# A diffusion layer's modulation: wider column blocks, another layout of the modulated streams, and earlier first loads

## The chip, the cores and the metric

The kernel runs on one core of a Trainium2 chip. The metric is the device time of one execution in microseconds, the median of several runs. Times of the profile come from one execution recorded by the hardware profiler. TensorE (PE in the profile, its weight loads PEld) does matmuls into PSUM; VectorE (DVE), ScalarE (ACT) and GpSimd (POOL) work on what lies in SBUF and, but for GpSimd, in PSUM. SP, ACT and POOL have queues of their own from which DMA transfers are issued, each in order.

## The reference, cut to what matters

One layer over 256 latent tokens `x` and 256 context tokens `ctx` of width 1024. Two conditioning vectors, `c` for the latent tokens and `c_ctx` for the context, give shift, scale and gate:

```python
mod_lat = jnp.split(jax.nn.silu(c) @ w_mod + b_mod, 6, axis=-1)      # w_mod: 1024 x 6144
mod_ctx = jnp.split(jax.nn.silu(c_ctx) @ w_mod + b_mod, 6, axis=-1)
sh1, sc1, g1, sh2, sc2, g2 = mod_lat
csh1, csc1, ... = mod_ctx
h_lat = rms_norm(x, norm_mix_g) * (1 + sc1) + sh1
h_ctx = rms_norm(ctx, norm_mix_g) * (1 + csc1) + csh1
y_lat = token_mixer(h_lat, h_ctx, ...)      # gated DeltaNet and GLA branches, both directions
x = x + g1 * y_lat
h = rms_norm(x, norm_ffn_g) * (1 + sc2) + sh2
x = x + g2 * moe_ffn(h, ...)                # top 4 of 32 experts, clamped SwiGLU
out = rms_norm(x, final_norm_g)
```

The first two vectors (`sh1`, `sc1`: columns 0 to 2047 of `w_mod`) are needed at once, for both streams. The other four (`g1`, `sh2`, `sc2`, `g2`: columns 2048 to 6143) are needed only after the mixer, and only for the latent stream.

## The kernel before, in words

All of it is float32; the projections run as three passes of fp32r halves. The program is written in the order of the layer, with two strings, ORDER1 and ORDER2, that give the order of the mixer's pieces by hand: `K0` is the DeltaNet key projection of head 0, `Pq0`, `Pk0`, `Pv0` are GLA projections, `U0` the GLA gates, `X0` the GLA attention, `V`, `Q`, `T`, `R` more of the same, and `M1` is one step of the rest of the modulation. A planner then orders the instructions of each engine and of each DMA queue: it takes the earliest in the program that its own costs say is ready. On the chip every engine and every queue runs in that order, and an instruction whose input is late holds all behind it.

**Beginning.** x and ctx are loaded, normalised and transposed (L218). The first modulation weights come in 16 loads of 512 KB, two halves `f` of eight k-tiles (L211), into a ring `wm` of eight buffers that the four `junk` tiles of the norm use too. Each load feeds two matmuls (L214) with the silu columns `sc` as stationary operand, 32 columns wide of which two are used; four column groups of the array take turns, so their sums lie in four groups of 32 rows of `pm`, and eight small matmuls with `sel` (L237) add them and turn them into columns `mc`. `modulate` (L167) then writes the modulated streams, 256 tokens each, as a high part (ScalarE, L171) and a low part (VectorE, L173 and L174) into `hT[0]` and `hT[1]`, with stream, k-tile and token as axes. Between the two halves stand three narrow loads of the low-rank projection (`wlr`, L226).

**Projections.** `wtake` loads 1024x128 weights into a ring of three buffers, `wsplit` makes the high and low halves on ScalarE and VectorE, and `passes` (L184) does 24 matmuls, of 512 columns where both streams are needed (K, V, Pk, Pv) and of 256 where only the latent one is.

**Rest of the modulation.** `wmod_next` (L849) is one step for 128 columns of `w_mod`: two loads of 256 KB from a ring `wm` of three buffers in the pool `ga`, eight matmuls with `sc` as stationary operand, four row groups of `pm`, a copy to SBUF by VectorE or ScalarE in turn, and in the next step a matmul with `sum4` (L879) that adds the four groups and turns the row into one column, which VectorE adds to the bias into `mod2` (L882, L884). There are 32 such steps, all in ORDER1.

**After that.** Closing `ga` makes room for `pD`, in which the DeltaNet's chunks are inverted (ORDER2); then the output projections, the router and the 32 experts, whose weights are prefetched into chunks as buffers come free.

Of the kernel before, what the change touches and what calls it, by code (L numbers as in the profile page):

```python
# [8 lines left out]
F32 = mybir.dt.float32  # L9
F32R = mybir.dt.float32r  # L10
# [3 lines left out]
AF = mybir.ActivationFunctionType  # L14
# [6 lines left out]
KT = 8  # L21
# [9 lines left out]
PF = (4, 0, 2, 0, 0, 1, 1, 0, 1, 0, 2, 1, 0)  # L31
DN = (0, 2, 1, 3)
HLB = (2, 2)
ORDER1 = "K0 Pq0 K1 Pk0 M1 U0 Pv0 Pv1 Pq1 Pk1 U1 M1 Pv2 M1 X0 M1 M1 M1 R0 M1 M1 K2 Pk2 Q0 M1 M1 Pq2 R1 M1 Pv4 M1 U2 Pq3 T0 M1 Pv3 X1 M1 M1 V0 Pv6 M1 Pv5 M1 T2 M1 T1 R2 M1 M1 Pk3 U3 V3 M1 V1 M1 Pv7 M1 X2 M1 R4 M1 K3 R3 M1 T3 V2 M1 R5 X3 Q1 Q2 R6 M1 M1 Q3 M1 R7 M1 M1"
ORDER2 = "A0 A0 G0 A0 A0 I0 I0 I0 I0 I0 I0 K4 G1 I0 K5 G3 G4 K6 G2 I0 G5 G6 K7 B0 B0 B0 B0 B0 B0 A1 T4 Q4 B0 A1 V4 Q6 V5 A1 A1 I1 T6 I1 T7 G7 I1 I1 T5 Z0 I1 I1 V6 H0 Q5 H1 Z1 I1 V7 I1 Q7 H2 B1 Z2 B1 B1 Z3 W0 B1 B1 B1 C1 Z4 Z5 H3 Z6 H4 B1 H5 H6 J0 Z7 Y0 Y1 Y2 H7 C1 Y3 C1"


# [1 line left out]
def hybrid_layer(ctx, tc, x, c, ctxt, c_ctx, w_mod, b_mod, norm_mix_g, norm_ffn_g, w_in, conv_w, a_log_f, a_log_b,  # L39
# [50 lines left out]
    big = open_pool("big")  # L90
    cst = open_pool("cst")
    lng = open_pool("lng")
    hT = [big.tile([128, 2, KT, 256], F32R, tag=f"hT{i}", name=f"hT{i}") for i in range(2)]
    xc = open_pool("xc")
    VA = xc.tile([16, 128], F32, name="VA")
    VR = xc.tile([96, 128], F32, name="VR")
    S.dma_start(VA[0:8], c[0].rearrange("(a p) -> a p", p=128))
# [2 lines left out]
    for src, tag in ((x, "yT"), (ctxt, "kA")):  # L100
        w = big.tile([128, 2, D], F32, tag=tag, name="xt" + tag)
        nc.sync.dma_start(w, src[0].rearrange("(t p) d -> p t d", p=128))
        xt += [w[:, 0], w[:, 1]]
    rows = [(b_mod[0], 24, 48), (norm_mix_g[0], 16, 8), (norm_ffn_g[0], 72, 8), (gla_gate_b_f[0], 80, 4),
            (gla_gate_b_b[0], 84, 4), (gla_norm_g[0], 88, 2), (gdn_norm_g[0], 90, 1)]
    for v_, r0, n in rows:
# [41 lines left out]
    xnT = [t_[:, k] for t_ in (big.tile([128, 4, 512], F32, tag=n, name="xn" + n) for n in ("yh", "yl")) for k in range(4)]  # L148
    rst = cst.tile([128, 4], F32, name="rst")
    for t in range(4):  # L150
        junk = xc.tile([128, D], F32, tag="wm", bufs=8, name=f"junk{t}")
        S.activation(junk, xt[t], AF.Square, accum_out=ss[:, t:t + 1])
    S.activation(rst, ss, AF.Ln, bias=epsc, scale=1.0 / D)
    S.activation(rst, rst, AF.Exp, scale=-0.5)
# [12 lines left out]
    def modulate(kt):  # L167
        hf_ = xc.tile([128, 512], F32, tag="hf", bufs=2, name=f"hf{kt}")
        for r in range(2):
            sl = slice(256 * r, 256 * r + 256)  # L170
            S.activation(hT[0][:, r, kt], xnT[kt][:, sl], AF.Identity, bias=mc[:, r, 0, kt:kt + 1],  # L171
                         scale=mc[:, r, 1, kt:kt + 1])
            V.tensor_scalar(hf_[:, sl], xnT[kt][:, sl], mc[:, r, 1, kt:kt + 1], mc[:, r, 0, kt:kt + 1], ALU.mult, ALU.add)  # L173
            V.tensor_sub(hT[1][:, r, kt], hf_[:, sl], hT[0][:, r, kt])  # L174

    def wraw(name):
        return lng.tile([128, KT, 128], F32, tag="w", bufs=3, name=name)
# [6 lines left out]
    def passes(p, hl, act, n, k0=0, k1=KT):  # L184


        for i, a in ((0, 0), (1, 0), (0, 1)):
            for kt in range(k0, k1):
                r = act[a][:, 0, kt] if n == 256 else act[a][:, :, kt]
                T.matmul(p if n == 256 else p.rearrange("p (a b) -> p a b", a=2), hl[i][:, kt], r,  # L190
                         start=i + a + kt == 0, stop=a == 1 and kt == KT - 1)

    def dense3(w, act, n, nm, then=None):
        hl = wsplit(w, nm)
# [12 lines left out]
    for f in range(2):  # L207
        pm = PJ([128, 512], f"pm0{f}")
        for kt in range(KT):
            w = xc.tile([128, 2, 512], F32, tag="wm", bufs=8, name=f"wm0{f}{kt}")  # L210
            nc.sync.dma_start(w, w_mod[0, kt * 128:(kt + 1) * 128, 0:2048].rearrange("p (s h n) -> p s h n", s=2, h=2)[:, :, f])  # L211
            for s in range(2):
                g_ = 32 * (2 * (kt % 2) + s)
                T.matmul(pm[g_:g_ + 32], sc[:, kt], w[:, s], start=kt < 2, stop=kt >= KT - 2)  # L214
            if f == 0:
                pt = TP([128, 512], f"xT{kt}")
                for t in range(4):
                    T.transpose(pt[:, 128 * t:128 * t + 128], xt[t][:, 128 * kt:128 * kt + 128], ident)  # L218
                V.tensor_copy(xnT[kt], pt)
            else:  # L220
                if kt == 3:

                    wl = wraw("wlr")
                    G.memset(wl, 0.0)
                    for c0, n, o in ((C_BETA, 16, 0), (C_A, 16, 32), (C_LR, 32, 64)):
                        nc.sync.dma_start(wl[:, :, o:o + n], w_in[0][:, c0:c0 + n].rearrange("(k p) n -> p k n", p=128))  # L226
                    lr = wsplit(wl, "lr")
                if kt >= 4:
                    modulate(kt - 4)
        if f:  # L230
            plr = PJ([128, 512], "plr")
            passes(plr, lr, hT, 512, 0, 4)
        mr = xc.tile([128, 512], F32, name=f"mr0{f}")
        V.tensor_copy(mr, pm)
        pt = TP([128, 4, 4], f"mt0{f}")
        for a in range(4):
            T.matmul(pt[:, a], mr[:, 128 * a:128 * a + 128], sel.rearrange("p s r -> p (s r)"), start=True, stop=True)  # L237
        fs = slice(4 * f, 4 * f + 4)
        V.tensor_tensor(mc[:, :, :, fs], pt.rearrange("p a (s r) -> p r s a", s=2),
                        vc[:, 24:40].rearrange("p (s a) -> p s a", s=2)[:, None, :, fs].to_broadcast([128, 2, 2, 4]), ALU.add)  # L240
        V.scalar_tensor_tensor(mc[:, :, 1, fs], mc[:, :, 1, fs], 1.0, vc[:, None, 16 + 4 * f:20 + 4 * f].to_broadcast([128, 2, 4]),
                               ALU.add, ALU.mult)
# [4 lines left out]
    for i in range(2):  # L247
        T.transpose(pt[:, i], CR[:, i], ident[0:108, 0:108])
    V.tensor_copy(cw.rearrange("p (t r) -> p t r", t=2), pt)
    close_pool("xc")  # L250

    alg = cst.tile([128, 16], F32, name="alg")
    dtb = cst.tile([128, 16], F32, name="dtb")
    for t_, pr in ((alg, (a_log_f, a_log_b)), (dtb, (dt_bias_f, dt_bias_b))):
        for i in range(2):
            nc.sync.dma_start(t_[:, 8 * i:8 * i + 8], dap(pr[i], 0, [[0, 128], [1, 8]]))

    def dense(src, col, act, n):
        return dense3(wtake(src, col), act, n, f"{src.tensor.name}{col}")

    def proj(col, n):
        return dense(w_in, col, late.get("hact", hT), n)

    passes(plr, lr, hT, 512, 4, KT)
    lrr = cst.tile([96, 512], F32, name="lrr")
# [521 lines left out]
    def spare(_):  # L787

        h1 = big.tile([128, KT, 256], F32R, tag="ra", name="hc1")
        S.copy(h1, hT[1][:, 0])  # L790
        mix = big.tile([128, 2, KT, 256], F32R, tag="hT1", name="mix")
        S.copy(mix[:, 0], hT[0][:, 0])
        late["mix"] = mix[:, 1]
        late["hact"] = mix[:, 0:1], h1[:, None]

# [43 lines left out]
    G.memset(gl_static["A"], 0.0)  # L839
    G.memset(gl_static["B"], 0.0)  # L840
    mod2 = keep.tile([128, 4, 8], F32, name="mod2")
    sum4 = cst.tile([128, 1], F32, name="sum4")
    V.tensor_reduce(sum4, ident[:, 0:128:32], AX.X, ALU.add)
    b1c = cst.tile([128, 8], F32, name="b1c")
    V.tensor_scalar_add(b1c, vc[:, 56:64], 1.0)

    wms = [0]

    def wmod_next(n):  # L849

        for _ in range(n):
            k, wms[0] = wms[0], wms[0] + 1
            col = 2048 + 128 * k
            if "pD" in gl_static:
                w = wtake(w_mod, col)
                w = w[:, 0:4], w[:, 4:8]
            else:
                w = [ga.tile([128, 4, 128], F32, tag="wm", bufs=3, name=f"wm{k}{i}") for i in range(2)]
                for i in range(2):
                    nc.sync.dma_start(w[i], w_mod[0][512 * i:512 * i + 512, col:col + 128].rearrange("(k p) n -> p k n", p=128))  # L860

            pt = GD([128, 128], f"pm{k}")
            for kt in range(KT):
                r = 32 * (kt % 4)
                T.matmul(pt[r:r + 32], sc[:, kt], w[kt // 4][:, kt % 4], start=kt < 4, stop=kt >= 4)
            mr = lng.tile([128, 256], F32, tag="sq", bufs=2, name=f"mr{k}")[:, 0:128]
            (S.copy if k % 2 else V.tensor_copy)(mr, pt)
            pend.append((k, mr))
            if k:
                wmod_sum()  # L870
            if k == 31:
                wmod_sum()

    pend = []

    def wmod_sum():
        k, mr = pend.pop(0)
        pc = GD([128, 1], f"pc{k}")
        T.matmul(pc, mr, sum4, start=True, stop=True)  # L879
        v_, b = (2, 0, 1, 3)[k // 8], k % 8  # L880
        if v_ == 1:
            V.scalar_tensor_tensor(mod2[:, 1, b:b + 1], pc, b1c[:, b:b + 1], vc[:, 72 + b:73 + b], ALU.add, ALU.mult)  # L882
        else:
            V.tensor_add(mod2[:, v_, b:b + 1], pc, vc[:, 40 + k:41 + k])  # L884


    slots = [("hT0", 0), ("hT0", 1), (big, "ra")]
# [71 lines left out]
    x1 = mo.tile([128, 2, D], F32, tag="x1", name="x1")  # L959
    nc.sync.dma_start(x1, x[0].rearrange("(t p) d -> p t d", p=128))  # L960
    wr = lng.tile([128, 8, NE], F32, name="wr")
    nc.sync.dma_start(wr, w_router[0].rearrange("(k p) n -> p k n", p=128))
    br = lng.tile([128, NE], F32, name="br")
    nc.sync.dma_start(br, dap(b_router, 0, [[0, 128], [1, NE]]))
    slots += [(mwA, f"m{i}") for i in range(1, NB1)] + [("hT1", 0), ("hT1", 1)]
    tw = []

# [384 lines left out]
```

## Time and profile before

| what | us |
|---|---|
| median of 3 runs | 1654.06 (1653.64 to 1654.14) |
| the profiled execution | 1650.16 |
| its span, first to last instruction | 1648.5 |
| TensorE busy in the span | 1450.1 (88%) |
| VectorE busy | 703.8 (43%) |
| ScalarE busy | 487.5 (30%) |
| mean granted TensorE clock | 0.975 of full |

A busy share over the whole span is an average over stages that have different limits. The stages are: the beginning up to about 60 us, the projections and GLA up to about 312, the DeltaNet up to about 560, its end and the merges, and from about 620 the experts with their weights. A matmul of float32 operands shows as two records in the profile, one for each pass.

### The profile page before, as it was taken

The page shows a single profiled execution, that of the slowest core. Times are in us where ns is not written, and L with a number is a line of the kernel's source. Part 1 is how long each engine was busy: PE and PEld are TensorE (multiplying, and loading weights), DVE is VectorE, ACT ScalarE, POOL GpSimd, SP SyncE. Part 2 cuts the span into 40 slices and gives each one's busy share as a digit, 9 for nine tenths or more (in the row PEclk, how much of TensorE's full clock was granted, in tenths as well). Part 3 has the DMA queues.
Part 4 walks back from the last instruction along what each step waited for, and adds up shares of the span by engine and source line. Part 5 has one row for each costly group of instructions (what it writes and reads, how often), then busy time and mean ns, then how long its engine had stood idle before and what let it go on. Part 6 is the DMA issues. An engine that isn't in the chain of part 4 may idle for free. (4 is left out here: it accounts for less than half of the span.)

```text
span 1648.5 us, 23441 instructions
## 1 busy us (share of the span) xinstructions
PE 1450.1 (88%) x9420; PEld 817.6 (50%) x9421; DVE 703.8 (43%) x1717; ACT 487.5 (30%) x994; POOL 15.0 (1%) x41
## 2 busy tenths in 40 slices
PE   5999999858977899899999988888989989889886
PEld 2677778747966898743433332433323223223221
DVE  4886676897799977422122111112111121121112
ACT  2555454745474654431111100101001011011011
POOL 1000000000000000000000000000000000000000
PEclk9999999978999999899999999999999999999999
DMA  9437444624223449799999999999999999999997
GB/s 299 120 104 193 122 135 129 173 57 124 77 78 104 143 133 314 263 381 415 417 415 416 417 414 409 381 415 416 417 414 417 416 415 417 417 415 417 415 417 296
DMA packets 223490, 491.86 MB, mean 298 GB/s; under 512 B 14706, under 2 KB 152248, under 8 KB 190576
## 3 DMA queue, kind: packets, MB, share of 16 engines
q1 hardware_dynamic: 221856, 486.02, 78.0%
q0 software_dynamic: 848, 3.30, 0.5%
q8 instruction: 76, 1.25, 0.3%
q10 hardware_dynamic: 672, 0.99, 0.2%
q14 instruction: 38, 0.31, 0.1%
HBM read 489.15 MB, written 1.11 MB: 297 GB/s over the span
## 5 line engine op out<-in xcount | busy, mean ns | idle before, releaser
L1076 PE MATMUL g<-w,xTm 128*64 128x512 f32 x1616 | 374.9, 599 | 37.7 <-DMA w<-in_w_gu_dram 35.8
L1076 PEld LDWEIGHTS g<-w,xTm 128*64 128x64 f32 x1616 | 105.9, 136 | 282.0 <-issue 165.2
L1151 DVE TENSOR_SCALAR glu<-g 128x256 f32<-128x256 f32 x64 | 24.3, 420 | 467.0 <-PE g L1076 467.0
L190 PE MATMUL pdin_w_in_dram<-hT,hiin_w_in_dram 128*128 128x256 f32 (+1 forms) x1008 | 204.3, 344 | 2.6 <-ACT hiin_w_in_dram L82 1.7
L1076 PE MATMUL pd<-w,aT 128*64 128x512 f32 x864 | 196.1, 598 | 0.0
L1152 ACT ACTIVATE sig<-glu 128x256 f32<-128x256 f32 x64 | 23.3, 409 | 503.3 <-DVE glu L1151 503.3
L190 PEld LDWEIGHTS pdin_w_in_dram<-hT,hiin_w_in_dram 128*128 128x128 f32 x1008 | 158.1, 194 | 27.0 <-issue 4.8
L1181 DVE SCALAR_TENSOR_TENSOR ys<-pd,pcm,grow 128x512 f32<-128x512 f32 x32 | 24.0, 751 | 246.7 <-PE pd L1076 246.7
L190 PE MATMUL pdin_w_in_dram<-hT,loin_w_in_dram 128*128 128x256 f32 (+1 forms) x504 | 107.8, 349 | 23.8 <-DVE loin_w_in_dram L83 23.8
L1076 PEld LDWEIGHTS pd<-w,aT 128*64 128x64 f32 x864 | 59.8, 137 | 113.6 <-issue 98.5
L1076 PE MATMUL g<-chT,xTm 128*64 128x512 f32 x432 | 102.5, 600 | 13.9 <-DMA chT<-in_w_gu_dram 13.2
L190 PEld LDWEIGHTS pdin_w_in_dram<-hT,loin_w_in_dram 128*128 128x128 f32 x504 | 80.7, 197 | 34.9 <-DVE loin_w_in_dram L83 25.3
L83 DVE TENSOR_TENSOR loin_w_in_dram<-win_w_in_dram,hiin_w_in_dram 128x1024 fp32r<-128x1024 f32 x72 | 87.7, 1220 | 15.0 <-ACT hiin_w_in_dram L82 14.9
L1183 ACT CAST ysig<-ys 128x512 fp32r<-128x512 f32 x32 | 19.8, 617 | 249.9 <-DVE ys L1181 249.9
L352 DVE SCALAR_TENSOR_TENSOR ra<-ra,cw 128x189 f32<-128x189 f32 (+2 forms) x192 | 80.6, 427 | 10.2 <-ACT ra L343 8.8
L82 ACT CAST hiin_w_in_dram<-win_w_in_dram 128x1024 fp32r<-128x1024 f32 x72 | 75.2, 1045 | 13.8 <-DMA win_w_in_dram<-in_w_in_dram 4.8
L1076 PEld LDWEIGHTS g<-chT,xTm 128*64 128x64 f32 x432 | 27.9, 136 | 78.4 <-issue 40.7
L1162 PE MATMUL pa<-ident,glu 128*128 128x128 f32 x128 | 26.6, 289 | 37.0 <-DVE glu L1155 32.5
L1076 PE MATMUL pxm<-ohm,xp 128*128 128x256 f32 x256 | 38.1, 306 | 9.7 <-DVE ohm L1086 7.9
L1076 PEld LDWEIGHTS pxm<-ohm,xp 128*128 128x128 f32 x256 | 34.8, 209 | 16.7 <-issue 8.6
L1162 PEld LDWEIGHTS pa<-ident,glu 128*128 128x128 f32 x128 | 12.8, 140 | 47.4 <-PE ppm L1076 22.2
L1076 PE MATMUL pd<-chT,aT 128*64 128x512 f32 x160 | 36.0, 592 | 0.0
(470 smaller groups left out, 1954.3 us busy)
## 6 DMA issues: line engine op xcount, KB each, us to landing
w<-in_w_gu_dram SPq DMA_DIRECT2D x200, 1024.0 KB, 20.0
w<-in_w_down_dram SPq DMA_DIRECT2D x106, 1024.0 KB, 20.0
chT<-in_w_gu_dram SPq DMA_DIRECT2D x54, 1024.0 KB, 19.9
win_w_in_dram<-in_w_in_dram SPq DMA_DIRECT2D x72, 512.0 KB, 4.2
chT<-in_w_down_dram SPq DMA_DIRECT2D x20, 1024.0 KB, 20.0
wm<-in_w_mod_dram SPq DMA_DIRECT2D x64, 256.0 KB, 3.6
wm<-in_w_mod_dram SPq DMA_DIRECT2D x16, 512.0 KB, 7.6
win_w_out_b_dram<-in_w_out_b_dram SPq DMA_DIRECT2D x8, 512.0 KB, 4.3
```

What stands on the lines that cost most here:

```text
L82: S.copy(hi, src)
L83: V.tensor_sub(lo, src, hi)
L190: T.matmul(p if n == 256 else p.rearrange("p (a b) -> p a b", a=2), hl[i][:, kt], r, start=i + a + kt == 0, stop=a == 1 and kt == KT - 1)
L352: V.scalar_tensor_tensor(al[:, r0:r1, q0:q1], rl[:, r0 + y - 1:r1 + y - 1, q0 + x_ - 1:q1 + x_ - 1], wc(y, x_), al[:, r0:r1, q0:q1], ALU.m ...
L1076: return tc.keep_in_program_order(T.matmul(*args, **kw))
L1151: V.tensor_scalar_min(gl_[:, cs], pg[0][:, cs], 7.0)
L1152: sig = S.activation(sg_[:, cs], gl_[:, cs], AF.Sigmoid, scale=1.702)
L1162: T.transpose(pt[:, a], gl_[:, 256 * c_ + 128 * a:256 * c_ + 128 * a + 128], ident))
L1181: V.scalar_tensor_tensor(ys, pd, pc, grow, ALU.mult, ALU.mult)
L1183: S.copy(yp[0], ys)
```

## The change

Four edits come together. The 16 first modulation loads get a pool `xw` with 16 buffers, on the right side, and stand in the program right behind the loads of x and ctx; `junk` gets a buffer of its own; six small loads (`alg`, `dtb`, `wr`, `br`) move from SP's queue to POOL's. The axes of `hT` become k-tile, stream, token, so that both streams' 512 columns of a k-tile lie side by side. `wmod_next` takes 512 columns in a step: eight loads of 256 KB, three buffers as before, eight matmuls of 512 columns, then a transpose of 32x32 blocks on VectorE (`mr`) of which every 32nd column is kept in `modT`; after the last step four matmuls with a wider `sum4` add the row groups of all steps at once, and five VectorE instructions write `mod2`. ORDER1 keeps 8 of its 32 `M1`, about every fourth, and is otherwise the same.

```diff
-ORDER1 = "K0 Pq0 K1 Pk0 M1 U0 Pv0 Pv1 Pq1 Pk1 U1 M1 Pv2 M1 X0 M1 M1 M1 R0 M1 M1 K2 Pk2 Q0 M1 M1 Pq2 R1 M1 Pv4 M1 U2 Pq3 T0 M1 Pv3 X1 M1 M1 V0 Pv6 M1 Pv5 M1 T2 M1 T1 R2 M1 M1 Pk3 U3 V3 M1 V1 M1 Pv7 M1 X2 M1 R4 M1 K3 R3 M1 T3 V2 M1 R5 X3 Q1 Q2 R6 M1 M1 Q3 M1 R7 M1 M1"
+ORDER1 = "K0 Pq0 K1 Pk0 U0 Pv0 Pv1 Pq1 Pk1 U1 M1 Pv2 X0 M1 R0 K2 Pk2 Q0 M1 Pq2 R1 Pv4 U2 Pq3 T0 Pv3 X1 M1 V0 Pv6 Pv5 T2 M1 T1 R2 Pk3 U3 V3 V1 M1 Pv7 X2 R4 K3 R3 M1 T3 V2 R5 X3 Q1 Q2 R6 Q3 M1 R7"
...
-    hT = [big.tile([128, 2, KT, 256], F32R, tag=f"hT{i}", name=f"hT{i}") for i in range(2)]
+    hT = [big.tile([128, KT, 2, 256], F32R, tag=f"hT{i}", name=f"hT{i}") for i in range(2)]
+    hL = [h[:, None, :, 0] for h in hT]
     xc = open_pool("xc")
+
+    xw = open_pool("xw", side="right")
+    wms0 = {}
+
+    def wmod0(f, kt):
+        w = wms0[f, kt] = xw.tile([128, 2, 512], F32, tag="wm", bufs=16, name=f"wm0{f}{kt}")
+        nc.sync.dma_start(w, w_mod[0, kt * 128:(kt + 1) * 128, 0:2048].rearrange("p (s h n) -> p s h n", s=2, h=2)[:, :, f])
...
         nc.sync.dma_start(w, src[0].rearrange("(t p) d -> p t d", p=128))
         xt += [w[:, 0], w[:, 1]]
+    for k in range(16):
+        wmod0(*divmod(k, KT))
...
-        junk = xc.tile([128, D], F32, tag="wm", bufs=8, name=f"junk{t}")
+        junk = xc.tile([128, D], F32, tag="junk", bufs=1, name=f"junk{t}")
...
-            S.activation(hT[0][:, r, kt], xnT[kt][:, sl], AF.Identity, bias=mc[:, r, 0, kt:kt + 1],
+            S.activation(hT[0][:, kt, r], xnT[kt][:, sl], AF.Identity, bias=mc[:, r, 0, kt:kt + 1],
...
-            V.tensor_sub(hT[1][:, r, kt], hf_[:, sl], hT[0][:, r, kt])
+            V.tensor_sub(hT[1][:, kt, r], hf_[:, sl], hT[0][:, kt, r])
...
-                r = act[a][:, 0, kt] if n == 256 else act[a][:, :, kt]
-                T.matmul(p if n == 256 else p.rearrange("p (a b) -> p a b", a=2), hl[i][:, kt], r,
-                         start=i + a + kt == 0, stop=a == 1 and kt == KT - 1)
+                r = act[a][:, 0, kt] if n == 256 else act[a][:, kt].rearrange("p a b -> p (a b)")
+                T.matmul(p, hl[i][:, kt], r, start=i + a + kt == 0, stop=a == 1 and kt == KT - 1)
...
-            w = xc.tile([128, 2, 512], F32, tag="wm", bufs=8, name=f"wm0{f}{kt}")
-            nc.sync.dma_start(w, w_mod[0, kt * 128:(kt + 1) * 128, 0:2048].rearrange("p (s h n) -> p s h n", s=2, h=2)[:, :, f])
+            w = wms0[f, kt]
...
-            nc.sync.dma_start(t_[:, 8 * i:8 * i + 8], dap(pr[i], 0, [[0, 128], [1, 8]]))
+            G.dma_start(t_[:, 8 * i:8 * i + 8], dap(pr[i], 0, [[0, 128], [1, 8]]))
...
-        return dense(w_in, col, late.get("hact", hT), n)
+        return dense(w_in, col, late.get("hact", hL) if n == 256 else hT, n)
...
-    sum4 = cst.tile([128, 1], F32, name="sum4")
-    V.tensor_reduce(sum4, ident[:, 0:128:32], AX.X, ALU.add)
+    sum4 = cst.tile([128, 32], F32, name="sum4")
+    V.tensor_reduce(sum4, ident.rearrange("p (g j) -> p j g", g=4), AX.X, ALU.add)
...
-            col = 2048 + 128 * k
...
+            col = 2048 + 512 * k
+
+            pt = GD([128, 512], f"pm{k}")
             for kt in range(KT):
+                w = ga.tile([128, 512], F32, tag="wm", bufs=3, name=f"wm{k}{kt}")
+                nc.sync.dma_start(w, w_mod[0][128 * kt:128 * kt + 128, col:col + 512])
                 r = 32 * (kt % 4)
...
+                T.matmul(pt[r:r + 32], sc[:, kt], w, start=kt < 4, stop=kt >= 4)
+
+            mr = ga.tile([128, 512], F32, tag="mr", bufs=1, name=f"mr{k}")
+            V.transpose(mr, pt)
+            V.tensor_copy(modT[:, k], mr[:, 0:512:32])
+            if k == 7:
+                pc = GD([128, 32], "pc")
+                mv = modT.rearrange("p k (b q) -> p q k b", q=4)
+                for q in range(4):
+                    T.matmul(pc[32 * q:32 * q + 32], sum4, mv[:, q], start=True, stop=True)
...
-    nc.sync.dma_start(wr, w_router[0].rearrange("(k p) n -> p k n", p=128))
+    G.dma_start(wr, w_router[0].rearrange("(k p) n -> p k n", p=128))
...
-    nc.sync.dma_start(br, dap(b_router, 0, [[0, 128], [1, NE]]))
+    G.dma_start(br, dap(b_router, 0, [[0, 128], [1, NE]]))
```

## Rows read from the trace of the kernel before

**Rows 1.** Stages: us, busy PE, PEld, DVE, ACT, POOL, clock, DMA share, GB/s

```profile
60.00:312.00 252.00, 246.21 (x1762) 193.16 (x1762) 182.04 (x450) 140.11 (x282) 0.92 (x3) 0.99 0.50 138
312.00:560.00 248.00, 196.71 (x2062) 176.46 (x2062) 219.06 (x508) 143.19 (x286) 3.16 (x5) 0.90 0.35 96
...
620.00:1640.00 1020.00, 909.19 (x4925) 371.43 (x4926) 220.36 (x555) 141.86 (x299) 3.27 (x11) 0.99 0.99 400
```

**Rows 2.** The same columns for two narrower stretches of the beginning

```profile
16.00:28.00 12.00, 11.65 (x61) 4.38 (x59) 5.35 (x8) 0.00 (x0) 0.00 (x0) 1.00 1.06 387
...
44.00:50.00 6.00, 4.44 (x20) 2.61 (x20) 4.75 (x14) 3.92 (x8) 0.00 (x0) 1.00 0.06 8
```

**Rows 3.** SP's queue in order of time: start, length, issues

```profile
1.84 0.54 SPq L256 DMA_DIRECT2D alg<-in_a_log_f_dram  x1
...
6.85 15.79 SPq L211 DMA_DIRECT2D wm<-in_w_mod_dram  x12
22.73 6.46 SPq L226 DMA_DIRECT2D wlr<-in_w_in_dram  x3
29.29 2.07 SPq L211 DMA_DIRECT2D wm<-in_w_mod_dram  x4
```

**Rows 4.** Timeline of the beginning: start, length, engine, line, what it writes and reads

```profile
10.48 0.18 DVE L145 TENSOR_TENSOR sc<-sg,vcc 128x16 f32<-128x16 f32 x1
...
14.69 1.92 PE L214 MATMUL pm<-wm,sc 128*32 128x512 f32 x4 [1.81 <-DMA wm<-in_w_mod_dram]
...
30.32 0.17 DVE L241 SCALAR_TENSOR_TENSOR mc<-mc,vc 128x8 f32<-128x8 f32 x1
...
42.37 1.07 PE L214 MATMUL pm<-wm,sc 128*32 128x512 f32 x8
...
45.88 0.16 DVE L241 SCALAR_TENSOR_TENSOR mc<-mc,vc 128x8 f32<-128x8 f32 x1
...
51.82 0.75 DVE L174 TENSOR_TENSOR hT<-hf,hT 128x256 fp32r<-128x256 f32 x2
```

**Rows 5.** TensorE's timeline at a step that comes in halves and a whole one

```profile
142.49 0.42 PE L865 MATMUL pm<-wm,sc 128*32 128x128 f32 x8
142.85 1.22 PE L190 MATMUL pdin_w_in_dram<-hT,hiin_w_in_dram 128*128 128x256 f32 x8
...
222.74 0.65 PE L865 MATMUL pm<-wm,sc 128*32 128x128 f32 x16
223.31 0.38 PE L879 MATMUL pc<-sum,mr 128*128 128x1 f32 x2
223.56 2.09 PE L190 MATMUL pdin_w_in_dram<-hT,hiin_w_in_dram 128*128 128x512 f32 x8
```

**Rows 6.** TensorE's timeline: matmuls of 512 columns, in groups, alone, and in fp32r

```profile
30.00 1.92 PE L214 MATMUL pm<-wm,sc 128*32 128x512 f32 x16
...
84.07 1.12 PE L368 MATMUL pn<-ra,ones 128*128 128x512 f32 x2
85.03 0.60 PE L399 MATMUL pgv<-ident,e 128*128 128x128 f32 x4
...
195.96 1.98 PE L190 MATMUL pdin_w_in_dram<-hT,loin_w_in_dram 128*128 128x512 f32 x8
197.78 0.39 PE L190 MATMUL pdin_w_in_dram<-hT,hiin_w_in_dram 128*128 128x512 f32 x1
```

**Rows 7.** Loads of L860: who waited (us, times), and time to landing

```profile
  PE pm L865: 3.2, 5
...
DMA to landing us min/median/max: 2.7/3.6/5.2
```

**Rows 8.** Line L865, the steps' matmuls: ns min/median/max, first and last start

```profile
L865 PE MATMUL pm<-wm,sc x512: 269/273/297, 74.0 to 310.9; 128*32 128x128 f32 x171
```

**Rows 9.** VectorE's groups by line: busy us, mean ns, idle time before them

```profile
L598 DVE STREAM_TRANSPOSE Lp<-Dg 128x1024 f32<-128x1024 f32 x2 | 4.0, 1988 | 0.0
...
L884 DVE TENSOR_TENSOR mod<-pc,vc 128x1 f32<-128x1 f32 x24 | 3.7, 156 | 12.1 <-PE pc L879 12.1
```

More of the change, by code (lines that the diff above doesn't have):

```diff
@@ L249, in hybrid_layer @@
     V.tensor_copy(cw.rearrange("p (t r) -> p t r", t=2), pt)
+    close_pool("xw")
     close_pool("xc")
@@ L789, in spare @@
         h1 = big.tile([128, KT, 256], F32R, tag="ra", name="hc1")
-        S.copy(h1, hT[1][:, 0])
+        S.copy(h1, hL[1][:, 0])
         mix = big.tile([128, 2, KT, 256], F32R, tag="hT1", name="mix")
-        S.copy(mix[:, 0], hT[0][:, 0])
+        S.copy(mix[:, 0], hL[0][:, 0])
         late["mix"] = mix[:, 1]
@@ L847, in hybrid_layer @@
     wms = [0]
+    modT = cst.tile([128, 8, 16], F32, name="modT")
     def wmod_next(n):
@@ L852, in wmod_next @@
             k, wms[0] = wms[0], wms[0] + 1
-            col = 2048 + 128 * k
[L854 to L862, printed above, removed]
+            col = 2048 + 512 * k
@@ L863, in wmod_next @@
+            pt = GD([128, 512], f"pm{k}")
             for kt in range(KT):
+                w = ga.tile([128, 512], F32, tag="wm", bufs=3, name=f"wm{k}{kt}")
+                nc.sync.dma_start(w, w_mod[0][128 * kt:128 * kt + 128, col:col + 512])
                 r = 32 * (kt % 4)
-                T.matmul(pt[r:r + 32], sc[:, kt], w[kt // 4][:, kt % 4], start=kt < 4, stop=kt >= 4)
-            mr = lng.tile([128, 256], F32, tag="sq", bufs=2, name=f"mr{k}")[:, 0:128]
-            (S.copy if k % 2 else V.tensor_copy)(mr, pt)
@@ L868, in wmod_next @@
[L868 to L884, printed above, removed]
+                T.matmul(pt[r:r + 32], sc[:, kt], w, start=kt < 4, stop=kt >= 4)
@@ new lines, in wmod_next @@
+            mr = ga.tile([128, 512], F32, tag="mr", bufs=1, name=f"mr{k}")
[6 more added lines that the diff above has]
+                    T.matmul(pc[32 * q:32 * q + 32], sum4, mv[:, q], start=True, stop=True)
+                for i, v_ in enumerate((2, 0, 1, 3)):
+                    c8 = slice(8 * i, 8 * i + 8)
+                    if v_ == 1:
+                        V.tensor_add(mod2[:, 1], pc[:, c8], b1c)
+                        V.tensor_mul(mod2[:, 1], mod2[:, 1], vc[:, 72:80])
+                    else:
+                        V.tensor_add(mod2[:, v_], pc[:, c8], vc[:, 40 + 8 * i:48 + 8 * i])
```

## The prediction

> **What bounds the kernel now.** I read the stages first [rows 1]. In 60 to 312 us TensorE is busy 246.2 of 252 us at full clock, VectorE 182 and ScalarE 140: work taken from or given to TensorE there moves the end of the stage. In 312 to 560 VectorE is the fuller one (219 of 248). From 620 on the DMA share is 0.99 at 400 GB/s: the experts' weights are a fixed number of bytes, so the end moves as the start of that flood moves, which the two stages ahead set. So I count any microsecond won or lost before 312 us as one at the end; I found no slack there that would swallow it.
>
> Next the beginning, in narrower stretches [rows 2]: in 16 to 28 us the DMA is full (387 GB/s), in 44 to 50 it moves 8 GB/s and TensorE is busy only 4.4 of 6. Then SP's queue [rows 3]: twelve of the sixteen first modulation loads go out between 6.85 and 22.6 us, then the three narrow pieces of the low-rank projection for 6.5 us, and only at 29.3 the last four. Then the chain they feed [rows 4]: the last matmul group of half 1 begins at 42.37, the columns `mc` of that half are ready at 46.04 (45.88 + 0.16), and hT is complete at 52.57 (51.82 + 0.75).
>
> Last, one modulation step [rows 5, 6] and what it waits for [rows 7, 8].
>
> **The change, part by part.** The profiled execution took 1650.16 us, its span 1648.5 and 1.66 around it. The median of the runs shown is 1654.06, 3.9 above; I make the sum on the profile and put the difference on the median.
>
> *First loads.* Eight buffers become sixteen apart from `junk`, so no load waits for a matmul, and all sixteen stand on SP right behind x and ctx, at about 1.84 us, where the first `alg` load stands now, instead of at 6.85 to 31.4. Six small loads move to POOL's queue (some 0.5 us each, as on SP in [rows 3]: 3 us there, where I see nothing late behind them). Sixteen loads of 512 KB are 8.4 MB, x and ctx 2.1 MB. At the 387 GB/s of [rows 2] that is 21.7 and 5.4 us; with data flowing from about 2.4 us (an estimate: x's load goes out just ahead of the 1.84 of `alg`) the last lands near 29.5. The low-rank and the first input-projection weights queue behind them on SP, and land near 33 and 35.
>
> Half 0 gains less than its loads do. Its first matmuls start at 14.69 and can't start before `sc` at 10.66 (10.48 + 0.18), and between 16 and 28 TensorE was busy 11.65 of 12 us with them and the 32 transposes [rows 2, 4]. So `mc` of half 0, ready at 30.48 now, comes 0 to 4 us earlier: I take 2, so 28.5. Half 1's last matmul comes near 30 instead of 42.4, its `mc` 3.7 us later as now (42.37 to 46.04): 33.7. Then VectorE is the limit. Four modulated k-tiles cost it 6.5 us (46.04 to 52.57), so eight cost 13; between them lie the low-rank split, the copy of half 1 and one more split, about 2.5 us. From 28.5 that ends at 44, instead of 52.6: **9 us earlier**. Below: 12, if half 0 moves by 4 and one split falls outside. Above: 4, if the low-rank weights, behind 10 MB now, or the planner's order on VectorE hold it up.
>
> *The rest of the modulation on TensorE.* Before: 32 steps, each 16 records of 128 columns (two passes of eight matmuls) and one column sum. Where both weight tiles are there, 16 records take 0.57 us (222.74 to 223.31); where they come in halves, 0.36 each (142.49 to 142.85); the sum holds TensorE 0.25 (223.31 to 223.56) [rows 5]. Of the 512 records [rows 8] 18 steps' stand whole and 14 steps' in halves: 18 x 0.57 + 28 x 0.355 = 20.2; 32 sums are 8.0 to 8.3; matmuls that found their weights not landed cost 3.2 [rows 7]. Together 31.6 us.
>
> After: 8 steps, each eight matmuls of 512 columns, four of which go to different 32-row groups of the result. One such matmul by itself holds TensorE 0.96 (the two passes from 84.07 to 85.03, a 512-column matmul of the l2 norm), but eight, two groups of four, take 1.92 (30.00): four together cost what one does [rows 6]. So a step costs 1.92 if each four run side by side, 7.7 if each runs alone: **15 to 61 us** in all. What decides is how many weight tiles lie ready, and there are three buffers for eight tiles of 256 KB. Three are loaded ahead; the fourth can be issued only when the first has been read, and lands 2.7 to 5.2 us later, 3.6 in the median [rows 7]. So a step naturally goes in three trains, 3 + 3 + 2, with two returns of the buffers between, in which TensorE does projections as now. Three whole trains are 2.9 us. The tiles of a returning train come one by one, at best 0.68 us apart (256 KB at 387 GB/s): where TensorE stands waiting that adds up to 2 x 0.68 in the second train and 0.68 in the third, 2.0; where it comes late, nothing. I take 1.2 between, nearer to the middle than to either end: 4.1 per step, 33 in all. Four final sums of 32 columns, at 0.25, add 1. So 34 against 31.6: **2.4 us lost**, with ends of -16 (15.4) and +30.
>
> The Trainium skill ("DMA: Bandwidth & Descriptors", Anatomy of one DMA) gives every transfer a fixed cost of about 2.0 us, whatever its size, beside bytes over 436 GB/s. It speaks against more, dependent loads per step; for 256 KB it makes an estimated 2.6 us, and the shortest landing in the trace, 2.7, agrees. By it two returns in each of eight steps would cost 42 us if nothing covered them, and the sum would be about 32 us worse than mine.
>
> *VectorE and ScalarE.* A step now ends in a 32x32-block transpose of 128x512 from PSUM and a small copy. The nearest row is the transpose of 128x1024 in SBUF, 1.99 us [rows 9]: 1.0 for half, with the copy 1.2 (the small column adds of now are 0.16), so 10 us in eight steps. What goes is 32 such adds, some 5 us, and half of 32 copies of 128 columns, about 4.6, as much; ScalarE loses the other half. Both have room in this stage [rows 1], so 0. If VectorE lost that cover the 10 us would count; it is replacing as much.
>
> *hT's layout.* A 512-column operand was two runs of 256, now one of 512. Eight such matmuls take 1.82 (195.96 to 197.78), 0.2275 each [rows 6]; 512 columns at the granted 2.4 GHz and one per cycle would be 0.213. At best this gives back 0.014 in 28 projections of 24, 672 matmuls: 9.6 us; no row shows that the two runs are what costs it, and the half-width projections are read as before, so 0. The two copies in `spare` read in wider steps, once.
>
> **Sum:** -9 + 2.4 = -6.6, say 7 us: profile 1643, **1647** on the median.
>
> **Rivals.**
> 1. *Slower: the trains break up.* If other matmuls fall between the returning tiles, each of the five runs alone: 0.96 + 5 x 0.96 = 5.8 per step, 47 with the final sums, 15 to 16 more than before; less 9 that is +6.5: 1661, and with all eight alone 1675. It decides from 5.1 us of TensorE per step, (31.6 + 9) / 8. For it: where one tile was outstanding before, the trace puts projections between the halves (142.85) [rows 5]. Against: a single 512-column matmul lasts 0.96, longer than the 0.68 between tiles, so the next tile is there when it ends.
> 2. *Much faster: trains come whole.* If TensorE always reaches them late, 8 x 2.9 + 1 = 24: -7.4, with the 9 (or up to 12) -16 to -19: 1636. For it: only 3.2 us of waiting now, in 64 loads [rows 7].
> 3. *The first loads don't help*, because hT waits for the low-rank weights or VectorE, or the order doesn't put the loads early: -3 + 2.4, about 1653. For it: VectorE already has 15 of the us to do after half 0; against: 42.37 is a wait for loads, and 44 to 50 is idle time on the DMA.
>
> **How the numbers follow.** My forecast, hT about 9 us earlier and a step of 3.5 to 4.8 us, gets 0.55; rival 1 0.20, rival 2 0.12, rival 3 0.13. About 0.2%, 3.3 us, can be told from no change. Below 1650.8 lie most of the forecast (0.48), rival 2 and a little of rival 3: faster 0.62. Within: 0.07 of the forecast, 0.10 of rival 3, 0.05 of rival 1: 0.22. Slower 0.16. The range goes from rival 2 to the milder half of rival 1: 1635 to 1661; the forecast's own is 1641 to 1653.
>
> **What would show it.** Right: all sixteen first loads issued by 12 us and landed by 31; hT complete at 42 to 46; eight steps of three trains each, TensorE 3.5 to 4.8 us in each with waits; the stage boundary that is at 312 near 305; the flood unchanged in length. Wrong: hT complete after 49; matmuls of 512 columns standing alone with 0.96 each between projections; waits of TensorE for modulation weights above 12 us in sum; VectorE waiting in its transposes so that the weight splits come late.

## The result, and the profile after

The change made the kernel slower by 0.6%: a median of 1661.51 us in 5 runs (1658.92 to 1666.74) against 1653.64 in 5 runs of before. The ratio, which like all ratios here rests on all the runs and not on the two medians, is 1.0062, interval 1.0038 to 1.0085. The median lies just beyond the predicted range of 1635 to 1661, at the time of its first rival, 1661. The profiled execution took 1661.38, its span 1659.7.

SP's queue of the changed kernel, in order of time (answers to [rows 3]):

```profile
1.84 23.08 SPq L102 DMA_DIRECT2D wm<-in_w_mod_dram  x16
25.48 9.20 SPq L235 DMA_DIRECT2D wlr<-in_w_in_dram  x3
34.73 6.81 SPq L213 DMA_DIRECT2D win_w_in_dram<-in_w_in_dram  x3
```

The end of its beginning: the last matmuls of half 1, that half's `mc`, the last low part of hT, and the low-rank matmuls (answers to [rows 4]):

```profile
33.63 1.05 PE L223 MATMUL pm<-wm,sc 128*32 128x512 f32 x4 [0.34 <-DMA wm<-in_w_mod_dram]
34.97 1.05 PE L223 MATMUL pm<-wm,sc 128*32 128x512 f32 x4 [0.29 <-DMA wm<-in_w_mod_dram]
...
38.45 0.16 DVE L250 SCALAR_TENSOR_TENSOR mc<-mc,vc 128x8 f32<-128x8 f32 x1
...
43.08 3.36 PE L201 MATMUL plr<-hT,hilr 128*128 128x512 f32 x8
...
44.38 0.75 DVE L185 TENSOR_TENSOR hT<-hf,hT 128x256 fp32r<-128x256 f32 x2
```

All 16 loads now stand right behind x and ctx, but their issue takes SP until 24.92 (1.84 + 23.08). hT is complete at 45.13 (44.38 + 0.75), 7.4 us before the 52.57 of [rows 4]. From there on the gain turns into a loss. The first `kk` matmul of the DeltaNet, in before and then in after (one execution each, as in all that follows from a trace):

```profile
311.81 2.03 PE L577 MATMUL kk<-kA 128*128 128x128 f32 x16
```

```profile
320.86 2.05 PE L587 MATMUL kk<-kA 128*128 128x128 f32 x16
```

9.0 us late there, 11.2 in the span; the flood is as long as it was (stages of after, columns as in [rows 1]):

```profile
60.00:320.00 260.00, 257.38 (x1289) 174.70 (x1288) 174.93 (x403) 133.82 (x260) 0.92 (x3) 1.00 0.46 133
...
631.00:1651.00 1020.00, 911.10 (x4919) 371.55 (x4919) 219.88 (x554) 142.17 (x299) 4.39 (x11) 0.99 0.99 400
```

So TensorE, full from 60 us on, has more to do. TensorE's timeline around one wide step shows what (answers to [rows 5]):

```profile
123.75 1.06 PE L871 MATMUL pm<-wm,sc 128*32 128x512 f32 x6
124.74 3.07 PE L201 MATMUL pdin_w_in_dram<-hT,hiin_w_in_dram 128*128 128x512 f32 x12
127.75 1.05 PE L871 MATMUL pm<-wm,sc 128*32 128x512 f32 x2
128.72 0.97 PE L201 MATMUL pdin_w_in_dram<-hT,hiin_w_in_dram 128*128 128x512 f32 x3
129.62 1.05 PE L871 MATMUL pm<-wm,sc 128*32 128x512 f32 x4
130.60 1.44 PE L201 MATMUL pdin_w_in_dram<-hT,loin_w_in_dram 128*128 128x512 f32 x5
131.97 1.04 PE L871 MATMUL pm<-wm,sc 128*32 128x512 f32 x2
132.94 0.97 PE L201 MATMUL pdin_w_in_dram<-hT,loin_w_in_dram 128*128 128x512 f32 x3
133.75 1.09 PE L201 MATMUL pdin_w_in_dram<-hT,hiin_w_in_dram 128*128 128x512 f32 x4
134.77 1.04 PE L871 MATMUL pm<-wm,sc 128*32 128x512 f32 x2
```

Two records are one matmul. The eight matmuls go as 3, 1, 2, 1 and 1, with projections between, and every group here holds TensorE the same 0.97 to 0.99, whether it has one, two or three in it: five such slots, 4.9 us. Six of the eight steps go like this; the fifth and the last go as 1, 2, 1, 2, 1 and 1, and two of the pairs take longer than a slot (281.44 and 311.65). Added up over TensorE's timeline from 60 us to `kk` (each group to the start of the next instruction, without the waits), the steps cost 42.7 us, with the final sums and waits for their weights 43.9. The 32 narrow steps, added up in the same way in before, cost 31.8. That is 12.1 us more; the matmuls themselves waited only 1.0 us for weights.

VectorE's two rows of a step (groups by line, answers to [rows 9]):

```profile
L874 DVE STREAM_TRANSPOSE mr<-pm 128x512 f32<-128x512 f32 x8 | 5.7, 716 | 12.5 <-PE pm L871 12.5
L875 DVE COPY modT<-mr 128x16 f32<-128x16 f32 x8 | 1.3, 166 | 0.0
```

### The profile page after: what moved, and what is told of

The parts are those of the page before. It is cut to its first block, busy times and chain, and to the rows that moved or that the text cites. A ratio compares the mean times of both kernels' runs of the same rounds, so it can differ in the third digit from the quotient of the medians.

```text
span 1659.7 us, 22493 instructions
## 1 busy us (share of the span) xinstructions
PE 1475.0 (89%) x8980; PEld 810.5 (49%) x8981; DVE 701.7 (42%) x1690; ACT 485.3 (29%) x978; POOL 19.7 (1%) x47
## 5 line engine op out<-in xcount | busy, mean ns | idle before, releaser
L82 ACT CAST hiin_w_in_dram<-win_w_in_dram 128x1024 fp32r<-128x1024 f32 x72 | 75.2, 1045 | 12.5 <-DMA gw<-in_gla_gate_w_f_dram 4.8
L1165 PE MATMUL pa<-ident,glu 128*128 128x128 f32 x128 | 26.6, 289 | 37.0 <-DVE glu L1158 32.4
L871 PE MATMUL pm<-wm,sc 128*32 128x512 f32 x128 | 45.5, 605 | 1.0 <-DMA wm<-in_w_mod_dram 1.0
```

The lines of the kernel that those rows point to most:

```text
L82: S.copy(hi, src)
L871: T.matmul(pt[r:r + 32], sc[:, kt], w, start=kt < 4, stop=kt >= 4)
L1165: T.transpose(pt[:, a], gl_[:, 256 * c_ + 128 * a:256 * c_ + 128 * a + 128], ident))
```

## The experiments

**Each edit alone.** `e1_first` is before with the first loads' edit, `e2_wide` before with the wide steps and the new ORDER1, `e3_layout` before with the new axes of `hT`.

> The kernel before with the first loads' edit alone: sixteen buffers, loads right behind the inputs, the six small loads on POOL's queue; narrow steps and the old layout stay. Theory A (the first loads gain what hT's completion shows, 45.1 us against 52.6, and the wide steps lose more): 6 to 8 us faster than before, ratio about 0.996. Rival B (the start's gain is swallowed later): within 2 us of before.

> The kernel before with the 512-column steps alone. Theory A (eight steps of five trains cost TensorE 43.9 us where the 32 narrow ones cost 31.8): 11 to 14 us slower, ratio about 1.007, its matmuls in the same broken trains (3, 1, 2, 1, 1 tiles). Rival C (the loss of the whole change is in the layout or in the order of the projections): at most 4 us slower.

> The kernel before with the new axes of hT alone. Theory A: 0, within 2 us. Rival C (512 columns in one run stream slower: eight matmuls in 1.87 to 1.88 us after the change against 1.82 before, over 84 such groups): 4 to 5 us slower.

| kernel | median us | ratio to before | interval | first `kk` |
|---|---|---|---|---|
| `e1_first` | 1650.29 | 0.9978 | 0.9965 to 0.9991 | 309.05 |
| `e2_wide` | 1663.82 | 1.0061 | 1.0045 to 1.0076 | 326.51 |
| `e3_layout` | 1651.14 | 0.9991 | 0.9982 to 1.0000 | 314.46 |

(Before: 1652.67 in 23 runs. The last column is from one execution each; that of `e3_layout` was its slowest of 12.) By the ratios the wide steps alone make the loss, 10 us where theory A had 11 to 14, in the same trains as after. The layout is worth at most 3 us. The first loads bring 3.6 us where 6 to 8 were expected, with hT 5 us earlier. The parts add to +5 us where the whole measured +10 (by the medians to 7 and 8); the intervals are wide enough for both, and the difference isn't settled.

**How the tiles arrive.** Four versions of the changed kernel differ in the modulation's loads alone: three one-tile buffers (after), six of them (`e4_six`), three buffers of two tiles with a load for each pair (`e10_pairs`), one buffer of four tiles with a load of 1 MB (`e5_quads`).

`e4_six`:

```diff
-                w = ga.tile([128, 512], F32, tag="wm", bufs=3, name=f"wm{k}{kt}")
+                w = ga.tile([128, 512], F32, tag="wm", bufs=6, name=f"wm{k}{kt}")
```

`e5_quads`; `e10_pairs` has the same form with four loads of two tiles and `bufs=3`:

```diff
-for kt in range(KT):
-    w = ga.tile([128, 512], F32, tag="wm", bufs=3, name=f"wm{k}{kt}")
...
+for i in range(2):
+    w = ga.tile([128, 4, 512], F32, tag="wm", bufs=1, name=f"wm{k}{i}")
+    nc.sync.dma_start(w, w_mod[0][512 * i:512 * i + 512, col:col + 512].rearrange("(k p) n -> p k n", p=128))
+    for j in range(4):
+        T.matmul(pt[32 * j:32 * j + 32], sc[:, 4 * i + j], w[:, j], start=i == 0, stop=i == 1)
```

> The changed kernel with one load of 1 MB for four k-tiles and one buffer of four tiles instead of three of one, so that four matmuls become ready together. Theory A (the trains break because tiles come one by one): each step is two trains of four, 1.92 us, about 15.5 in all instead of 43.9, so 25 to 28 us faster than the change and 14 to 18 faster than before, ratio about 0.990, less what TensorE waits for the larger loads. Rival D (the steps' cost on TensorE is not what the end follows): as the change, 1.006.

> After with six one-tile buffers in place of three. Theory A (a step's price is the number of separate trains, and that follows from how many tiles lie ready when the step begins): six ready tiles go as 4 + 2, the last two as one or two more, so 3 to 4 slots of 0.98 instead of 5: the steps take 24 to 32 us of TensorE instead of 42.7, and the whole is 10 to 17 us under after, ratio to before 0.990 to 0.997. Theory B (tiles that come by a load each run alone whatever lies ready): steps stay at 40 us or more, ratio 1.004 to 1.007.

> After with a load of 512 KB for each pair of k-tiles, three buffers of a pair. Theory A: three pairs lie ready, they go as 4 + 2, the fourth pair as one slot: 3 slots, 24 us of TensorE for all steps, ratio to before 0.988 to 0.993, the same as six one-tile buffers where those get their 3 slots, better where those split their last two. Theory B (only the size of a load counts, two tiles side by side at best): 4 slots, 32 us, 0.996 to 0.999.

The line of the steps' matmuls, by groups: busy us, mean ns of one | idle time before them. In after, `e4_six`, `e10_pairs` and `e5_quads`:

```profile
L871 PE MATMUL pm<-wm,sc 128*32 128x512 f32 x128 | 45.5, 605 | 1.0 <-DMA wm<-in_w_mod_dram 1.0
```

```profile
L871 PE MATMUL pm<-wm,sc 128*32 128x512 f32 x128 | 34.3, 602 | 1.4 <-DMA wm<-in_w_mod_dram 1.3
```

```profile
L872 PE MATMUL pm<-wm,sc 128*32 128x512 f32 x128 | 26.0, 602 | 3.4 <-DMA wm<-in_w_mod_dram 3.4
```

```profile
L871 PE MATMUL pm<-wm,sc 128*32 128x512 f32 x128 | 18.1, 605 | 5.8 <-DMA wm<-in_w_mod_dram 5.8
```

128 records of 0.60 us each in all four, and busy times that fall as more of them lie side by side.

| kernel | groups of most steps | us on TensorE, added up | first `kk` | median us | ratio to before, interval |
|---|---|---|---|---|---|
| after | 3, 1, 2, 1, 1 | 42.7 | 320.86 | 1661.51 | 1.0062 (1.0038 to 1.0085) |
| `e4_six` | 6, 1, 1 (four slots) | 32.4 | 309.69 | 1650.82 | 0.9984 (0.9975 to 0.9994) |
| `e10_pairs` | 6, 2 (three slots) | 24.7 | 303.58 | 1643.48 | 0.9942 (0.9928 to 0.9957) |
| `e5_quads` | 4, 4 (two slots) | 16.9 | 298.20 | 1635.59 | 0.9894 (0.9878 to 0.9909) |

A slot less per step is 8 to 10 us less on TensorE and 7 to 11 in the median, while the waits grow only from 1.0 to 5.8. Theory B falls in both, and `e5_quads` came as its theory A had it. Theory A of the other two had the slots and TensorE's time, but its ratios were too good: 0.990 to 0.997 for `e4_six`, 0.988 to 0.993 for `e10_pairs`. `e5_quads` is 17 us faster than before, with the same arithmetic as the change. In its timeline a step is two groups of four (eight records), each in one slot:

```profile
120.76 1.07 PE L871 MATMUL pm<-wm,sc 128*32 128x512 f32 x8
...
127.34 1.07 PE L871 MATMUL pm<-wm,sc 128*32 128x512 f32 x8
```

TensorE's order is fixed before the run, so the groups are the planner's, made by its own costs: the trains of after stand in `e2_wide` too, and in the fifth step one matmul goes ahead alone in all four versions, in `e5_quads` as well, where one load brings all four tiles:

```profile
192.49 1.04 PE L871 MATMUL pm<-wm,sc 128*32 128x512 f32 x2
...
194.05 1.06 PE L871 MATMUL pm<-wm,sc 128*32 128x512 f32 x6
```

So the loads decide the groups by way of the order that the planner makes for them. Whether an order that waits for its tiles would do as well with one-tile loads, no run shows.

**What the first loads are worth.** `e9_nofirst` is `e5_quads` with the first loads and the small loads as in before. `e8_late` is `e5_quads` with the router's loads late; `e12_late_between` is `e8_late` with the low-rank loads again between the halves.

`e8_late` (`br` in the same way):

```diff
-    G.memset(gl_static["A"], 0.0)
+    ast_ = G.memset(gl_static["A"], 0.0)
...
-    G.dma_start(wr, w_router[0].rearrange("(k p) n -> p k n", p=128))
+    with tc.issue_after(ast_.ins):
+        G.dma_start(wr, w_router[0].rearrange("(k p) n -> p k n", p=128))
```

`e12_late_between`, besides that (the same four lines leave the loop over `f`):

```diff
     for k in range(16):
+        if k == 8:
+            wl = lng.tile([128, KT, 128], F32, tag="w", bufs=3, name="wlr")
+            G.memset(wl, 0.0)
+            for c0, n, o in ((C_BETA, 16, 0), (C_A, 16, 32), (C_LR, 32, 64)):
+                nc.sync.dma_start(wl[:, :, o:o + n], w_in[0][:, c0:c0 + n].rearrange("(k p) n -> p k n", p=128))
         wmod0(*divmod(k, KT))
```

> The version with one load for four k-tiles, but with the first loads and the six small loads as before. If the first loads are worth what they were worth alone, it is 2.5 to 4 us slower than with them: ratio 0.991 to 0.992 against 0.989. If their 7 us at hT count in full once the steps are cheap, 0.994. If they are worth nothing there, 0.989 to 0.990.

> The version with one load for four k-tiles, and the router's two loads (wr 128 KB, br 16 KB) put behind a memset on POOL at about 45 us. Theory A (small packets in the burst cost DMA time): 12 to 18 us moves over 330 GB/s instead of 230 to 280, the last modulation matmul of half 1 comes 1.5 to 2.5 us earlier and hT with it; in the end 0.5 to 2 us, ratio 0.988. Theory B (the rate there has another cause, x and ctx or the conv weights): rate and hT unchanged, 0.9895.

> The version with one load for four k-tiles and the router's loads late, and the three narrow low-rank loads put back between the two halves of the first modulation weights. Theory A (the first loads gained little because TensorE had only some 7 us of idle time between 28 and 60 us, part of it covered by low-rank matmuls that ran while half 1 was awaited; only that idle time can be won): half 1 and hT come 2 to 4 us later, the low-rank matmuls of half 0 start before half 1's last matmul again, and the end moves by less than 1.5 us: ratio 0.988 to 0.990. Theory B (every microsecond at hT is one at the end): 2 to 4 us slower than without, 0.990 to 0.991.

`e9_nofirst`: 1637.53, ratio 0.9903 (0.9885 to 0.9921), against 0.9894 with them: 1.5 us, not told apart from nothing or from 4; the 7.0 us by which its hT is later (53.05 against 46.04) would make 0.9936, outside its interval. `e8_late`: 1634.69, 0.9886 (0.9869 to 0.9903). The rate in 12 to 18 us rose from 234 to 269 GB/s, not to the 330 expected; half 1's last group started 2.7 us earlier (33.22 instead of 35.88) and hT was complete 1.2 earlier; the time can't be told from `e5_quads`. `e12_late_between`, on another chip and against before there: 1635.84, 0.9891 (0.9874 to 0.9908). Its hT is complete at 51.49, and in `e8_late` at 44.86 (VectorE's timeline, `e12_late_between` first):

```profile
50.74 0.75 DVE L190 TENSOR_TENSOR hT<-hf,hT 128x256 fp32r<-128x256 f32 x2
```

```profile
44.11 0.75 DVE L185 TENSOR_TENSOR hT<-hf,hT 128x256 fp32r<-128x256 f32 x2
```

Their first `kk`, in the same order:

```profile
295.68 2.05 PE L587 MATMUL kk<-kA 128*128 128x128 f32 x16
```

```profile
296.87 2.05 PE L587 MATMUL kk<-kA 128*128 128x128 f32 x16
```

So the 6.6 us at hT don't come through in full: that would make 0.9926, outside the interval. Theory B, which is the prediction's own step, falls in that sense; between theory A's 1.5 us and the 2 to 4 that B was put at, the times don't decide. The traces show where the microseconds go. I counted the projection matmuls, the low-rank ones among them, in pairs of kernels whose hT lies apart:

| later hT, earlier hT | hT apart, us | 100th projection matmul apart | first `kk` apart |
|---|---|---|---|
| before, after | 7.4 | 3.7 | (wide steps between) |
| before, `e1_first` | 5.0 | 2.3 | 2.8 |
| `e9_nofirst`, `e5_quads` | 7.0 | 3.4 | 1.2 |
| `e12_late_between`, `e8_late` | 6.6 | 2.8 | -1.2 |

About half is gone at the 100th, by 68 us at the latest. In the last pair what is left then goes too, in waits for weights of the modulation (4.5 us in `e8_late`, 2.3 in `e12_late_between`) and most of it at 141 us, where `e8_late` waits longer and then runs at a granted clock of 0.50 (142 to 144 us) against 1.00 (`e8_late` first):

```profile
141.23 1.53 PE L871 MATMUL pm<-wm,sc 128*32 128x512 f32 x8 [1.85 <-DMA wm<-in_w_mod_dram]
142.69 4.16 PE L201 MATMUL pdin_w_in_dram<-hT,hiin_w_in_dram 128*128 128x256 f32 x16
```

```profile
143.02 1.07 PE L871 MATMUL pm<-wm,sc 128*32 128x512 f32 x8 [1.09 <-DMA wm<-in_w_mod_dram]
144.02 3.09 PE L206 MATMUL pdin_w_in_dram<-hT,hiin_w_in_dram 128*128 128x256 f32 x16
```

One execution of each can't tell whether this always happens, so it is not shown that nothing at all is left at the end. For the first half the stretch 28 to 60 us gives a reason, which is argued and not set apart by a run (columns as in [rows 1]; before, after, `e8_late`, `e12_late_between`):

```profile
28.00:60.00 32.00, 24.52 (x125) 14.28 (x122) 21.82 (x66) 14.23 (x26) 0.88 (x3) 0.95 0.68 183
```

```profile
28.00:60.00 32.00, 28.46 (x141) 19.73 (x142) 25.35 (x79) 16.06 (x31) 0.87 (x3) 0.89 0.61 171
```

```profile
28.00:60.00 32.00, 28.71 (x142) 20.84 (x143) 24.80 (x78) 16.06 (x31) 2.27 (x5) 0.84 0.64 177
```

```profile
28.00:60.00 32.00, 27.91 (x128) 15.44 (x128) 21.74 (x70) 13.56 (x27) 2.26 (x5) 0.89 0.66 200
```

TensorE was idle for 7.5 us of these 32 in before, 3.5 in after, 3.3 and 4.1 in the other two. No more than the idle time can be won there. In before and in `e12_late_between` the low-rank matmuls of half 0 run while half 1's loads are awaited (35.55 to 42.37 us in before); with all loads ahead they come only after half 1's last matmul (from 37.52 in `e8_late`), and part of them runs at half the clock. The first of them in before:

```profile
35.55 1.65 PE L190 MATMUL plr<-hT,hilr 128*128 128x512 f32 x3 [3.63 <-ACT hilr L82]
```

**The clock.** `e14_fill` is `e8_late` with 24 transposes that nothing reads, behind `modulate`.

```diff
     for kt in range(4, KT):
         modulate(kt)
+    for k in range(6):
+        pt = TP([128, 512], f"fill{k}")
+        for t in range(4):
+            T.transpose(pt[:, 128 * t:128 * t + 128], xnT[0][:, 128 * t:128 * t + 128], ident)
```

> The version with one load for four k-tiles and the router's loads late, and 24 extra transposes of 128x128, whose results nothing reads, placed in the program behind the modulation of half 1, so that TensorE has work while it waits for hT. Theory A (part of what an earlier hT brings is lost because TensorE then works at half the clock): granted clock of 36 to 44 us at 0.9 or more instead of 0.50, the low-rank matmuls 0.24 us each instead of 0.45, the first kk 1 to 2 us earlier than 296.9, ratio 0.987 to 0.988. Theory B (the clock falls in spite of it, or the extra work stands in front of the modulated tiles): clock below 0.8, kk at 297 or later, 0.988 to 0.990.

1632.34, ratio 0.9868 (0.9852 to 0.9884), the lowest of all, 21 us under before; the interval overlaps that of `e8_late`. Windows of 36 to 44 us in `e8_late`, then in `e14_fill`:

```profile
36.00:44.00 8.00, 6.64 (x20) 5.14 (x21) 6.26 (x18) 4.98 (x9) 0.00 (x0) 0.50 0.50 138
```

```profile
36.00:44.00 8.00, 7.72 (x42) 7.07 (x43) 6.78 (x20) 5.93 (x10) 0.00 (x0) 0.79 0.60 168
```

The clock is at 0.79 instead of 0.50. Eight low-rank matmuls in a row cost 3.37 us in `e8_late` (42.81 to 46.18) and 1.94 in `e14_fill` (42.04 to 43.98):

```profile
42.81 3.54 PE L201 MATMUL plr<-hT,hilr 128*128 128x512 f32 x8
```

```profile
42.04 1.17 PE L201 MATMUL plr<-hT,lolr 128*128 128x512 f32 x4
43.05 1.10 PE L201 MATMUL plr<-hT,hilr 128*128 128x512 f32 x4
```

Theory A's clock of 0.9 or more did not come, and 0.79 is what theory B allowed; the first `kk`, at 293.52, is 3.35 earlier than in `e8_late` and against theory B. But in the other executions with early loads and no such transposes the same stretch has 0.66 (`e4_six`), 0.67 (`e10_pairs`), 0.70 (after), 0.83 (`e5_quads`) and 0.95 (`e1_first`), so one execution doesn't show that the transposes raised it. And the 60th projection matmul starts only 0.2 us earlier (55.79 against 56.00); 1.7 of the 3.35 us arose at 141 to 146 us, where `e8_late` ran at half the clock and `e14_fill`, after a wait of 1.71 us, did not. What the transposes are worth is open.

## Why the prediction was wrong, point by point

- **The wide steps: the step that failed.** I took 4.1 us per step and 2.4 lost in all; 5 slots in most steps, 42.7 us and 12.1 lost is what the trace has. The rule "four side by side cost what one costs" held, and so did "what decides is how many weight tiles lie ready". What failed is "a step naturally goes in three trains, 3 + 3 + 2". In six of the eight steps only the first train came whole, in two not even that. Its three buffers come free together, but the next load is used alone at 127.75, 3.0 us after that train's end, and projections follow it in TensorE's fixed order. The tile which comes next finds TensorE in them, and its buffer is returned late in turn. My argument against rival 1, that 0.96 is longer than the 0.68 between tiles, presumed that TensorE goes from one tile to the next; the order put 3 to 12 projection matmuls there instead, as it already did at 142.85 [rows 5]. Rival 1 named the mechanism with 5.8 us per step; it was 5.3 (42.7 / 8), just beyond its turning point of 5.1. That point counted on the 9 us of the first loads; with the 3.6 that they brought it lies at 4.4, (31.8 + 3.6) / 8. Four versions with 5, 4, 3 and 2 slots in most steps settle that the slots are the price.
- **Waits for the weights.** TensorE and its weight loads waited 6.1 us for them in all (1.0 + 5.1), under my bound of 12. So the price wasn't paid in waiting. The 42 us for uncovered returns, worked out from the Trainium skill ("DMA: Bandwidth & Descriptors", Anatomy of one DMA), did not arise. The Trainium skill's figure is for transfers that GpSimd issues; on SP's queue the loads' shortest landing, 2.5 us, agrees with the estimate of 2.6, the median is 3.1. Two long loads per step, `e5_quads`, are what paid.
- **The first loads.** hT came 7.4 us earlier, inside the ends of 4 to 12 but under the 9 I took; 45.13 lies in the window of 42 to 46. Half 1's last group started at 34.97, not near 30, and the 16 loads were not issued by 12 us: they took SP 23 us, at 252 GB/s in 12 to 18 us (before: 344) and 362 in the 16 to 28 us for which [rows 2] has 387. Half 0's `mc` came 0.4 us earlier (30.09) where I took 2, half 1's at 38.61 where I had 33.7, so hT followed the loads and not VectorE. The 6.5 us that I gave VectorE for four k-tiles held a split of weights already (47.38 in before, 1.22 us). The worse error is the sentence "I count any microsecond won or lost before 312 us as one at the end". At hT it doesn't hold: the edit alone gave 3.6 us (1.5 to 5.8) for 5.0 at hT, and of 5.0 to 7.4 us at hT about half was left at the 100th projection matmul in four pairs of kernels. The two errors, 9.7 us in the steps and 5.4 in the first loads, make 15 of the 17 us between the forecast's -6.6 and the +10 of the ratio. Rival 3 had this in part, for another reason.
- **The late part of the chain.** From `kk` on it holds to about 2 us: 9.0 there, 11.2 in the span, the flood unchanged.
- **VectorE, ScalarE: 0, right.** The transpose took 0.72 us, with the copy 0.88, where I had 1.2. It waited 12.5 us for `pm`, and no split of weights was late for it: TensorE's wait for the low part of 512-column weights fell from 2.2 to 0.7 us. A small reading was off: 19 of the narrow steps came whole and 13 in halves, not 18 and 14, which moves the 20.2 us by under 1.
- **hT's layout: 0, right.** 0.9991, nearer to 0 than to the -9.6 at best.

## What to carry to other kernels

Matmuls that fill only a column group of the array are cheap only in company, so load their operands as one transfer that makes the whole company ready at once; more bytes per load were worth more here than more loads in flight. When an input is made to come earlier, count the idle time of the bounding engine behind it, and the work that the old wait covered: that, and not the distance at the input, is what can be won (here about half of it). Where an engine's order is planned ahead, other work is put in front of a tile that the plan doesn't count on yet, and a buffer ring with less than a step's tiles then returns its buffers one by one.

## What the runs showed of the hardware

- A queue doesn't take 16 loads of 512 KB at once: single issues on SP lasted up to 3.08 us, and the load behind them had to wait for 25.48. The burst was slower with the router's loads of 144 KB in it, on POOL's queue: in 12 to 18 us five executions with them moved 227 to 263 GB/s at a DMA share of 1.03 to 1.04, two without them and else alike (`e8_late`, `e14_fill`) 269 and 299. Their bytes alone would be 24 GB/s of that.
- TensorE ran at half of its clock (1.2 of 2.4 GHz) between 40 and 46 us of after (0.50, 5.0 of 6 us busy), behind a stretch from 36 to 40 with gaps in which it was busy 2.7 of 4 us. In 36 to 44 us the granted clock lay between 0.50 and 0.95 in the six executions with early loads in which TensorE had much the same to do, so a loss by the clock in one trace need not be in the next.
- Eight 512-column matmuls in groups of 6 and 2 held TensorE three slots (`e10_pairs`): two of the 6 go to a column group that is in use already, and the 6 took 1.91 us where 4 take 1.07.
